# A hybrid encoder layer in float32: seven buffers for the gate's embedding terms, constants in the rows of a weight, squares of x behind its high parts

## The chip, the cores and the metric

The kernel runs on one core of one Trainium2 chip. The metric is the device time of one execution in microseconds (us). The engines are TensorE (PE in the profile, its weight loads PEld), VectorE (DVE), ScalarE (ACT), GpSimd (POOL) and SyncE (SP, which only issues DMAs here).

## The reference, cut to what matters

Sequence 1024, width 1024, one layer. `x` is the residual stream, `p` a per-layer embedding of width 256.

```python
h = rms_norm(x, pre_norm_gain)
q, k, v, z_a, b_gate, c_gate, u, z_c = split(h @ w_in, 8)      # eight parts of 512
attn = diff_attention(q, k, v, lam, slopes)                    # 4 heads, two softmax maps each
attn = rms_norm(attn, subln_gain) * 0.8 * silu(z_a)
conv_out = b_gate * conv3(c_gate * u) * silu(z_c)
mixed = concat(attn, conv_out) @ w_out
x = x + rms_norm(mixed, post_norm_gain)
e = rms_norm(p @ w_ple_proj, ple_norm_gain)
x = x + sigmoid(x @ w_ple_gate) * e
```

## The kernel before, in words

Everything is held transposed: rows of a tile are 128 of the 1024 features (a block `kt` or `m`), its columns 512 positions (a half `n`). Every large product is made in three passes of TensorE: each operand is split into a rounded high part (a cast on ACT, line 89 or 92) and the rest (a subtraction on DVE or POOL, line 90 or 93), and `mm3` (lines 99 to 102) adds high by high, high by rest and rest by high in PSUM. A product of one 128-wide block of outputs with one half of the positions is 8 x 3 = 24 matmuls of 512 columns.

**Order of the work.** The program is written in stages, and a scheduler of the compiler, with a model of the engines' times, sets the order of the instructions on each engine and queue from it: what is written first goes first when its operands are there by the model. On the chip each engine then keeps that order and waits at the head of its queue.

**First stage** (lines 290 to 350). PE runs nine matmuls of zeros. Three pieces of `w_ple` (blocks 0, 1 to 3 and 4 to 7; `load_ple`, line 304) and the two halves of `p` (`load_p`, line 309) are loaded by SP into the pool `rawp`, which has three buffers under the tag `raw`, and split. `embed(n)` multiplies them: 8 blocks of 6 matmuls per half, 96 in all, each block evacuated by ACT (odd `m`, line 326) or DVE (even `m`, line 328) and stored to `e_dram`. A small array of constants (18.5 KB, gains and convolution weights) is loaded by line 343 into `sm`; the splits of x need its columns. `load_x(n)` (line 299) loads the eight blocks of x of a half and splits them, scaled with `col(C_PRE, kt)`, into `hT`; `splits[n, kt]` keeps the two instructions. Then come the weights `wq` and `wk` of head 0 from `w_in`, through `raw` buffers too. Weights lie in the pool `wp`, three buffers under the tag `w` (line 125).

**Second stage.** `row_scale(n)` (line 366) squares the eight blocks of x on ACT (lines 359 and 362, tile `sqx`), adds them on DVE (line 363), sums over the rows with a small matmul (`column_sums`, lines 105 to 117, tile `ms`) and takes the inverse root on POOL (line 97, tile `rsx`); the result `R[n]` is spread over the rows by DVE (line 120). Products of `hT` with a weight are made before the scale is known; their evacuations multiply by `R[n]`. `run` at lines 376 to 378 makes q and k for half 0 (PSUM tag `p`, two banks), q and k for half 1 (tag `s`, three banks) and then the gate z with tag `p` again.

**Middle.** The values, four heads of attention interleaved with the convolution's products (`PLAN`), and `embed_scale`, which leaves the inverse roots for e in `rs_e`.

**Last stage** (from line 486). `out_half(m, n)` multiplies by `w_out`, `post(n, r)` norms, adds x and splits the result into `x1`. `gate_half(m, n)` (line 545), 16 times, loads `e` (line 550, back from `e_dram`, tag `e`, three buffers), scales it on DVE (line 551), multiplies `w_gate` by `x1` on PE (24 matmuls; for the last one two pieces of 256 columns), takes the tanh on ACT (line 560, tile `tg`, two buffers), forms `e = (tg + 1) * e` and `e = e + mix` on DVE (lines 561, 562) and stores `e` from SP to the output (line 563). A buffer of `e` is free for the next load when its store has landed.

Of the kernel before, what the change touches and what calls it, by code (L numbers as in the profile page):

```python
# [12 lines left out]
F32 = mybir.dt.float32  # L13
F32R = mybir.dt.float32r
# [6 lines left out]
P = 128  # L21
# [3 lines left out]
KT = D // P  # L25
HALF = 512
# [14 lines left out]


@with_exitstack
def hybrid_layer(ctx, tc, xT, pT, w_in, small, lams, w_out, w_ple, w_gate, outT):
    nc = tc.nc
    V, A, T, G = nc.vector, nc.scalar, nc.tensor, nc.gpsimd
    mult, add, sub = ALU.mult, ALU.add, ALU.subtract
# [4 lines left out]
    wp = ctx.enter_context(tc.tile_pool(name="wp", bufs=3))  # L52
    rawp = ctx.enter_context(tc.tile_pool(name="rawp", bufs=3))
# [15 lines left out]
    def bank_t(name):  # L69
        return ps_s.tile([P, HALF], F32, tag="t", bufs=2, name=name)  # L70
# [7 lines left out]
    sm = small_c[:, 20:57]  # L78
# [5 lines left out]
    def col(base, k):  # L84
        return sm[:, base + k:base + k + 1]

    def split(hi, lo, src, scale=None, lo_eng=None):
        if scale is None:
            A.copy(out=hi, in_=src)  # L89
            (lo_eng or V).tensor_tensor(out=lo, in0=src, in1=hi.bitcast(F32), op=sub)  # L90
        else:
            return (A.activation(out=hi, in_=src, func=AF.Copy, scale=scale),
                    V.scalar_tensor_tensor(out=lo, in0=src, scalar=scale, in1=hi.bitcast(F32), op0=mult, op1=sub))
# [61 lines left out]
    with ExitStack() as st:  # L155
# [134 lines left out]
        with ExitStack() as st0:  # L290
            sp = st0.enter_context(tc.tile_pool(name="sp", bufs=1))
            s2 = st0.enter_context(tc.tile_pool(name="s2", bufs=2))

            wph = sp.tile([P, KT, 2, P], F32R, name="wph")
            wpo = sp.tile([P, KT, 2, P], F32R, name="wpo")

            splits = {}

            def load_x(n):
                for kt in range(KT):  # L300
                    nc.sync.dma_start(out=mix[kt][n], in_=xT[n, kt])
                    splits[n, kt] = split(hT[n][kt][:, 0], hT[n][kt][:, 1], mix[kt][n], col(C_PRE, kt))

            def load_ple(c):
                raw = rawp.tile([P, c.stop - c.start, 2, P], F32, tag="raw", name="rawe")
                nc.sync.dma_start(out=raw, in_=w_ple[:, c])
                split(wph[:, c], wpo[:, c], raw)

            def load_p(n):
                pth = s2.tile([P, 2, HALF], F32R, tag="pth", name="pth")  # L310
                pto = s2.tile([P, 2, HALF], F32R, tag="pto", name="pto")
                raw = rawp.tile([P, 2, HALF], F32, tag="raw", name="rawt")
                for k in range(2):
                    nc.sync.dma_start(out=raw[:, k], in_=pT[:, n, k])
                    split(pth[:, k], pto[:, k], raw[:, k])
                return pth, pto

            def embed(n, p):
                pth, pto = p
                for m in range(KT):  # L320
                    ps = bank_t("ple") if m % 3 else ps_a.tile([P, HALF], F32, tag="a", name="ple")
                    for k in range(2):
                        mm3(ps, wph[:, m, k], wpo[:, m, k], pth[:, k], pto[:, k], k == 0, k == 1)
                    e = s2.tile([P, HALF], F32, tag="e", bufs=5, name="e")
                    if m % 2:
                        A.copy(out=e, in_=ps)
                    else:
                        V.tensor_copy(out=e, in_=ps)
                    nc.sync.dma_start(out=e_dram[n, m], in_=e)


            zero = sp.tile([P, HALF], mybir.dt.bfloat16, name="zero")
            V.memset(zero, 0.0)
            idle = bank_p("idle")
            for _ in range(9):
                T.matmul(out=idle, lhsT=zero[:, :P], rhs=zero, start=True, stop=True)
            load_ple(slice(0, 1))
            pt0 = load_p(0)
            load_ple(slice(1, 4))
            load_ple(slice(4, 8))  # L340
            pt1 = load_p(1)
            embed(0, pt0)
            nc.sync.dma_start(out=sm, in_=small)
            V.tensor_scalar(out=subg, in0=sm[:, C_SUB:C_SUB + 1], scalar1=0.4, scalar2=None, op0=mult)
            load_x(0)
            embed(1, pt1)
            mixing_weight()
            wq = w_in_tile(0, 0, V)
            wk = w_in_tile(1, 0, V)
            load_x(1)  # L350


        with ExitStack() as st0:
            vp = st0.enter_context(tc.tile_pool(name="vp", bufs=1, reuse_waits="tile"))
            v2 = st0.enter_context(tc.tile_pool(name="v2", bufs=2, reuse_waits="tile"))

            def sums_x(n):
                acc = R[n]
                A.activation(out=acc, in_=mix[0][n], func=AF.Square)
                for kt in range(1, KT):  # L360
                    sq = rowp.tile([P, HALF], F32, tag="t", name="sqx")
                    A.activation(out=sq, in_=mix[kt][n], func=AF.Square)
                    V.tensor_tensor(out=acc, in0=acc, in1=sq, op=add)
                return acc

            def row_scale(n):
                r = tiny.tile([P, 16], F32, tag="rs", name="rsx")
                rsqrt(r, column_sums(sums_x(n), rowp, tag="t")[:, :16], D, 1e-6)
                spread(R[n], r)
                for g in range(4):  # L370
                    A.copy(out=r_col[32 * g:32 * g + 32, 4 * n:4 * n + 4], in_=r[32 * g:32 * g + 32, g:16:4])

            head0 = Head(0)
            row_scale(0)
            row_scale(1)
            run([(wq, head0.ev_q), (wk, head0.ev_k)], (0,))
            run([(wq, head0.ev_q), (wk, head0.ev_k)], (1,), bank_s)
            run([(w_in_tile(3, 0, V), head0.ev_z)])
            wv = vp.tile([P, 2, KT, HALF], F32R, name="wv")
            for h in range(H):  # L380
                raw = rawp.tile([P, KT, P], F32, tag="raw", name="raw")
                nc.sync.dma_start(out=raw, in_=w_in[8 + h])
                c = slice(h * P, (h + 1) * P)
                split(wv[:, 0, :, c], wv[:, 1, :, c], raw)
            for j in range(NT):
                c = slice(j % 4 * P, j % 4 * P + P)
                ps = bank_p("v")
                for kt in range(KT):
                    b = hT[j // 4][kt]
                    mm3(ps, b[:, 0, c], b[:, 1, c], wv[:, 0, kt], wv[:, 1, kt], kt == 0, kt == KT - 1)  # L390
                v = v2.tile([P, 2, HALF], F32R, tag="v", name="v")
                split(v[:, 0], v[:, 1], ps, r_col[:, j:j + 1])
                nc.sync.dma_start(out=v_dram[j], in_=v.bitcast(F32))
# [64 lines left out]
        for h in range(H):  # L458
# [5 lines left out]
            for step in PLAN[h]:  # L464
                k, v = step[0], step[1:]
# [20 lines left out]
    with ExitStack() as st:  # L486
        cp = st.enter_context(tc.tile_pool(name="cp", bufs=1, reuse_waits="tile"))
        c2 = st.enter_context(tc.tile_pool(name="c2", bufs=2, reuse_waits="tile"))
        c4 = st.enter_context(tc.tile_pool(name="c4", bufs=4, reuse_waits="tile"))
# [55 lines left out]
        def gate_half(m, n):  # L545
            if len(re) == n:
                re.append(cp.tile([P, HALF], F32, name=f"re{n}"))
                spread(re[n], rs_e[:, 16 * n:16 * n + 16])
            e = c4.tile([P, HALF], F32, tag="e", bufs=3, name="e")
            nc.sync.dma_start(out=e, in_=e_dram[n, m])  # L550
            V.scalar_tensor_tensor(out=e, in0=e, scalar=col(C_PLE, m), in1=re[n], op0=mult, op1=mult)  # L551
            w = weight(KT + m)
            pieces = 2 if (m, n) == (KT - 1, 1) else 1
            step = HALF // pieces
            for c0 in range(0, HALF, step):
                c, o = slice(c0, c0 + step), slice(n * HALF + c0, n * HALF + c0 + step)
                ps = bank()[:, :step]
                product(w, [[b[:, :, c] for b in r] for r in x1], n, ps)
                t = c2.tile([P, HALF], F32, tag="tg", name="tg")[:, :step]
                A.activation(out=t, in_=ps, func=AF.Tanh, scale=0.5)  # L560
                V.scalar_tensor_tensor(out=e[:, c], in0=t, scalar=1.0, in1=e[:, c], op0=add, op1=mult)
                V.tensor_tensor(out=e[:, c], in0=e[:, c], in1=mix[m][n][:, c], op=add)
                nc.sync.dma_start(out=outT[m * P:(m + 1) * P, o], in_=e[:, c])
# [12 lines left out]
        for m in range(1, 6):  # L576
            gate_half(m, 0)
# [42 lines left out]
```

## Time and profile before

| | us |
|---|---|
| runs (3) | 650.86, 652.25, 652.95; median 652.25 |
| the profiled execution: its own time | 651.04 |
| the profiled execution: span from first to last instruction | 649.3 |
| PE busy | 631.8 (97% of the span) |
| DVE busy | 447.8 (69%) |
| ACT busy | 243.7 (38%) |
| POOL busy | 227.0 (35%) |
| granted clock of TensorE, mean | 0.995 of 2.4 GHz |

A busy share is that of the whole span. Matmuls overlap in the pipeline, so the length of one in the profile is more than the distance from one to the next; the distance is what counts for a stream of them. Times in rows are from the start of the span, and a row names the line of the kernel, the tile written and the tiles read.

### The profile page before, as it was taken

To read this page: it belongs to the slowest core of one execution; us is meant where nothing else is said; L and a number is where in the kernel's file an instruction comes from. 1 tells how busy PE (TensorE), PEld (TensorE's weight loads), DVE (VectorE), ACT (ScalarE), POOL (GpSimd) and SP (SyncE) were. 2 spreads that over 40 slices of the span, in tenths; PEclk is the share of its full clock that TensorE was granted. 3 is DMA by queue.
4 is the path that set the end of the run, shared out by engine and by line. 5 is a ranking of instruction groups with operands and counts; after the bars stand their busy time and mean duration, and the time that the engine had idled before them with its cause. 6 is when DMAs were issued, how large, how long until landed. Compare 5 with 4: busy or idle time off the path is not lost.

```text
span 649.3 us, 8064 instructions
## 1 busy us (share of the span) xinstructions
PE 631.8 (97%) x2941; PEld 523.2 (81%) x2941; DVE 447.8 (69%) x821; ACT 243.7 (38%) x442; POOL 227.0 (35%) x114
## 2 busy tenths in 40 slices
PE   7899999999999999999999999999999999999992
PEld 4688888888888888888888888888888888888882
DVE  6968512698786687876886999539881199795233
ACT  6945312334463333543444434114632326231110
POOL 2006100325326544256362132424560379450000
PEclk9999999999999999999999999999999999999997
DMA  8976522310254102352012400113140125143222
GB/s 286 383 279 194 195 86 86 92 58 5 82 145 138 44 34 81 103 158 65 33 49 82 130 33 33 65 34 130 65 163 0 34 73 187 33 145 98 93 86 97
DMA packets 35654, 67.77 MB, mean 104 GB/s; under 512 B 3744, under 2 KB 12448, under 8 KB 35616
## 3 DMA queue, kind: packets, MB, share of 16 engines
q1 hardware_dynamic: 35616, 67.27, 31.5%
q8 instruction: 23, 0.38, 0.2%
q14 instruction: 15, 0.12, 0.1%
HBM read 48.38 MB, written 12.58 MB: 94 GB/s over the span
## 4 chain that ended last, share of the span: by engine, by line
PE 71%; DVE 12%; DMA 9%; ACT 3%; issue 2%; POOL 2%; DVEq 0%; POOLq 0%; ACTq 0%
PE pj L100 14%; PE pj L102 14%; PE pj L101 14%; PE s L237 5%; DMA e<-e_dram 4%; DMA out_dram<-e 3%; DVE mix L539 3%; PE o L102 3%; PE o L100 3%; PE o L101 3%; PE tpw L264 2%; PE v L100 2%; PE v L101 2%; PE v L102 2%; DVE x L90 2%
## 5 line engine op out<-in xcount | busy, mean ns | idle before, releaser
L100 PE MATMUL pj<-hT,w 128*128 128x512 f32 x448 | 176.4, 394 | 1.2 <-ACT w L89 1.2
L101 PE MATMUL pj<-hT,w 128*128 128x512 f32 x448 | 176.2, 393 | 0.0
L102 PE MATMUL pj<-hT,w 128*128 128x512 f32 x448 | 176.1, 393 | 0.0
L90 POOL TENSOR_TENSOR w<-raw,w 128x1024 fp32r<-128x1024 f32 x41 | 105.5, 2582 | 146.6 <-ACT w L89 143.8
L100 PEld LDWEIGHTS pj<-hT,w 128*128 128x128 f32 x448 | 84.2, 188 | 18.1 <-ACT w L89 2.0
L102 PEld LDWEIGHTS pj<-hT,w 128*128 128x128 f32 x448 | 84.2, 188 | 16.4
L101 PEld LDWEIGHTS pj<-hT,w 128*128 128x128 f32 x448 | 84.2, 188 | 16.1
L245 ACT ACTIVATE p<-p,nm 128x128 f32<-128x128 f32 (+7 forms) x64 | 49.4, 772 | 70.6 <-DVE nm L241 60.7
L89 ACT CAST w<-raw 128x1024 fp32r<-128x1024 f32 x44 | 45.9, 1048 | 21.2 <-issue 11.6
L102 PE MATMUL o<-x,w 128*128 128x512 f32 (+1 forms) x136 | 51.3, 377 | 0.0
L100 PE MATMUL o<-x,w 128*128 128x512 f32 (+1 forms) x136 | 51.2, 377 | 0.0
L101 PE MATMUL o<-x,w 128*128 128x512 f32 (+1 forms) x136 | 51.2, 377 | 0.0
L100 PE MATMUL o<-mT,w 128*128 128x512 f32 x128 | 49.8, 389 | 0.0
L101 PE MATMUL o<-mT,w 128*128 128x512 f32 x128 | 49.8, 389 | 0.0
L102 PE MATMUL o<-mT,w 128*128 128x512 f32 x128 | 49.7, 390 | 0.0
L237 PE MATMUL s<-ks,qs 128*128 128x512 f32 (+2 forms) x192 | 47.5, 346 | 0.0
L89 ACT CAST wt<-tpw 128x512 fp32r<-128x512 f32 (+3 forms) x48 | 21.1, 479 | 60.1 <-PE tpw L264 60.0
L90 DVE TENSOR_TENSOR wt<-tpw,wt 128x512 fp32r<-128x512 f32 (+3 forms) x48 | 25.3, 551 | 26.2 <-ACT wt L89 26.1
L551 DVE SCALAR_TENSOR_TENSOR e<-e,small_c,re 128x512 f32<-128x512 f32 x16 | 16.3, 1017 | 36.5 <-DMA e<-e_dram 36.5
L241 DVE CUSTOM_DVE_ANT_0 p<-s,bias 128x512 f32<-128x512 f32 (+3 forms) x64 | 34.8, 564 | 9.3 <-PE s L237 5.4
L237 PEld LDWEIGHTS s<-ks,qs 128*128 128x128 f32 x192 | 33.4, 188 | 5.0
L405 POOL TENSOR_TENSOR mix<-mix,R 128x512 f32<-128x512 f32 x8 | 12.3, 1543 | 68.6 <-DVE mix L404 66.4
(139 smaller groups left out, 1117.6 us busy)
## 6 DMA issues: line engine op xcount, KB each, us to landing
raw<-in_w_in SPq DMA_DIRECT2D x32, 512.0 KB, 3.6
mix<-in_xT SPq DMA_DIRECT2D x16, 256.0 KB, 6.6
e_dram<-e SPq DMA_DIRECT2D x16, 256.0 KB, 5.6
mix<-e_dram SPq DMA_DIRECT2D x16, 256.0 KB, 3.1
ks<-ks SPq DMA_DIRECT2D x16, 256.0 KB, 3.5
v_dram<-v SPq DMA_DIRECT2D x8, 512.0 KB, 2.6
vs<-v_dram SPq DMA_DIRECT2D x32, 128.0 KB, 2.7
raw<-in_w_out SPq DMA_DIRECT2D x8, 512.0 KB, 3.2
```

Of the source, the lines that this page charges most:

```text
L89: A.copy(out=hi, in_=src)
L90: (lo_eng or V).tensor_tensor(out=lo, in0=src, in1=hi.bitcast(F32), op=sub)
L100: T.matmul(out=ps, lhsT=ah, rhs=bh, start=first, stop=False)
L101: T.matmul(out=ps, lhsT=ah, rhs=bl, start=False, stop=False)
L102: T.matmul(out=ps, lhsT=al, rhs=bh, start=False, stop=last)
L237: T.matmul(out=banks[m][:, :nn], lhsT=s.qs[:, m, qi], rhs=s.ks[:, m, part, c], start=part == 0, stop=part == 1)
L241: V.tensor_tensor_reduce(out=pr[m][:, c0:c0 + n], in0=banks[m][:, :n], in1=s.bias[:, b0:b0 + n], scale=-1.0, scalar=low[m], op0=add, op1=A ...
L245: A.activation(out=pr[m][:, :W], in_=pr[m][:, :W], func=AF.Exp, scale=-1.0, bias=low[m], accum_out=l[:, m:m + 1])
L264: T.transpose(out=tp[:, ii * P:(ii + 1) * P], in_=s.ws[ii][:, j * P:(j + 1) * P], identity=ident)
L405: G.tensor_tensor(out=o, in0=o, in1=R[n], op=mult)
L539: V.scalar_tensor_tensor(out=o, in0=o, scalar=col(C_POST, kt), in1=S1, op0=mult, op1=mult)
L551: V.scalar_tensor_tensor(out=e, in0=e, scalar=col(C_PLE, m), in1=re[n], op0=mult, op1=mult)
```

## The change

It has four parts. The tag `e` gets seven buffers in place of three. The first piece of `w_ple` is loaded on ACT's DMA queue instead of SP's. The constants no longer have an array and a load of their own: they are 37 more columns in the rows of the second piece of `w_ple`, from where DVE copies them to `sm`. The raw halves of `p` no longer take buffers of `raw`; both halves lie in one buffer of the tag `w`. `load_p(1)` is written behind `embed(0, pt0)`. And the instructions of `row_scale(n)` that run on ACT are tied behind `splits[n, KT - 1][0]`, the cast of the last high part of x of that half.

```diff
-            def load_ple(c):
-                raw = rawp.tile([P, c.stop - c.start, 2, P], F32, tag="raw", name="rawe")
-                nc.sync.dma_start(out=raw, in_=w_ple[:, c])
-                split(wph[:, c], wpo[:, c], raw)
+            def load_ple(c, o, queue=nc.sync, constants=0):
+                n = (c.stop - c.start) * 2 * P
+                raw = rawp.tile([P, n + constants], F32, tag="raw", name="rawe")
+                queue.dma_start(out=raw, in_=w_ple[:, o:o + n + constants])
+                if constants:
+                    V.tensor_copy(out=sm, in_=raw[:, n:])
+                split(wph[:, c], wpo[:, c], raw[:, :n].rearrange("p (a b c) -> p a b c", b=2, c=P))
...
-                raw = rawp.tile([P, 2, HALF], F32, tag="raw", name="rawt")
+                raw = p_raw[:, n].bitcast(F32).rearrange("p (k a) b -> p k (a b)", k=2)
...
-            load_ple(slice(0, 1))
+            p_raw = wp.tile([P, 2, KT, P], F32R, tag="w", name="p_raw")
+            load_ple(slice(0, 1), 0, nc.scalar)
             pt0 = load_p(0)
-            load_ple(slice(1, 4))
-            load_ple(slice(4, 8))
+            load_ple(slice(1, 4), 256, constants=37)
+            load_ple(slice(4, 8), 1024 + 37)
+            embed(0, pt0)
             pt1 = load_p(1)
-            embed(0, pt0)
-            nc.sync.dma_start(out=sm, in_=small)
...
-            row_scale(0)
-            row_scale(1)
+            for n in range(2):
+                with tc.issue_after(splits[n, KT - 1][0].ins):
+                    row_scale(n)
...
-            e = c4.tile([P, HALF], F32, tag="e", bufs=3, name="e")
+            e = c4.tile([P, HALF], F32, tag="e", bufs=7, name="e")
...
-        "small": c(small),
...
-        "w_ple": c(blocks(w_ple_proj).transpose(1, 0, 2, 3)),
+        "w_ple": c(np.concatenate([ple[:, :1024], small, ple[:, 1024:]], axis=1)),
```

`ple` is `w_ple_proj` in the same blocks as before, laid out as 128 rows of 2048 columns.

## Rows read from the trace of the kernel before

**Rows 1.** Windows: from:to, length, busy us (count) by engine, PEclk, DMA share, GB/s

```profile
637.52:649.30 11.78, 0.00 (x0) 0.00 (x0) 4.35 (x9) 0.77 (x2) 0.00 (x0) 0.70 0.30 111
...
5.83:25.73 19.90, 16.81 (x64) 11.50 (x65) 18.34 (x34) 18.05 (x31) 0.00 (x0) 1.00 1.01 364
25.73:637.52 611.79, 611.55 (x2869) 510.57 (x2867) 423.05 (x773) 222.60 (x407) 222.53 (x105) 1.00 0.29 95
```

**Rows 2.** The chain that ended last, its end: start, us, what

```profile
637.13 1.99 DMA out_dram<-e
639.13 2.54 DMA e<-e_dram
...
641.80 0.75 DVE e L551
...
645.64 0.42 DVE e L562
```

**Rows 3.** Waits, whole span: engine, line, releaser: us in total, times, longest

```profile
DVE e L551 <- DMA e<-e_dram: 36.5, 11, 4.2
...
DVE acc L523 <- ACT sqo L522: 24.8, 6, 4.7
```

**Rows 4.** Timeline of ACT, last stage: start, us, instruction [idle before it]

```profile
610.03 0.60 ACT L560 ACTIVATE tg<-o 128x512 f32<-128x512 f32 x1 [4.84 <-PE o L102]
615.48 0.60 ACT L560 ACTIVATE tg<-o 128x512 f32<-128x512 f32 x1 [4.84 <-PE o L102]
...
637.80 0.38 ACT L560 ACTIVATE tg<-o 128x256 f32<-128x256 f32 x1 [5.40 <-DVE e L561]
```

**Rows 5.** Timeline of DVE, start of the last stage

```profile
467.52 2.88 DVE L551 SCALAR_TENSOR_TENSOR e<-e,small_c,re 128x512 f32<-128x512 f32 x1
...
481.57 0.74 DVE L551 SCALAR_TENSOR_TENSOR e<-e,small_c,re 128x512 f32<-128x512 f32 x1
```

**Rows 6.** Timeline of POOL, the same stretch

```profile
462.27 18.82 POOL L90 TENSOR_TENSOR w<-raw,w 128x1024 fp32r<-128x1024 f32 x7 [9.77 <-ACT w L89]
```

**Rows 7.** Waits of PE, whole span

```profile
PE ple L100 <- ACT e L326: 1.1, 2, 0.9
...
PE pj L100 <- ACT w L89: 1.2, 2, 0.7
```

**Rows 8.** Windows of line 362 alone (ACT): squares of x before head 0's weights

```profile
8.77:23.70 14.93, 4.37 (x7) 1.00 1.02 376
```

**Rows 9.** Timeline of SP, first stage: start and length of DMA issues

```profile
0.72 0.39 SPq L306 DMA_DIRECT2D rawe<-in_w_ple  x1
1.17 0.90 SPq L314 DMA_DIRECT2D rawt<-in_pT  x2
```

**Rows 10.** Windows of the first stage, columns as in the first group

```profile
4.00:6.00 2.00, 0.82 (x4) 0.27 (x2) 1.49 (x6) 0.62 (x1) 1.00 (x1) 1.00 1.03 271
...
8.00:10.00 2.00, 1.50 (x7) 0.83 (x6) 1.32 (x3) 2.00 (x3) 0.00 (x0) 1.00 1.01 395
```

**Rows 11.** Timeline of DVE, first and second stage

```profile
8.15 0.15 DVE L344 TENSOR_SCALAR small_c<-small_c 128x1 f32<-128x1 f32 x1 [0.59 <-DMA small_c<-in_small]
...
9.71 0.68 DVE L328 COPY e<-ple 128x512 f32<-128x512 f32 x1
...
18.17 0.69 DVE L90 TENSOR_TENSOR pto<-rawt,pth 128x512 fp32r<-128x512 f32 x1
...
35.06 0.68 DVE L109 TENSOR_REDUCE part<-flip 128x16 f32<-128x512 f32 x1
...
53.74 0.68 DVE L194 SCALAR_TENSOR_TENSOR tq<-pj,R 128x512 f32<-128x512 f32 x1
```

**Rows 12.** Timeline of ACT: the third weight's cast

```profile
31.71 1.05 ACT L89 CAST w<-raw 128x1024 fp32r<-128x1024 f32 x1 [0.44 <-DMA raw<-in_w_in]
```

**Rows 13.** Timeline of PE, second stage: the sum over the rows

```profile
46.59 0.29 PE L116 MATMUL ms<-part,fold 128*128 128x16 f32 x2
```

**Rows 14.** Tile pj, 20 to 70 us: duration ns min/median/max, first and last start

```profile
L102 PE MATMUL pj<-hT,w x48: 389/389/476, 26.2 to 65.9; 128*128 128x512 f32 x48
```

More of the change, by code (lines that the diff above doesn't have):

```diff
@@ L43, in hybrid_layer @@
 @with_exitstack
-def hybrid_layer(ctx, tc, xT, pT, w_in, small, lams, w_out, w_ple, w_gate, outT):
+def hybrid_layer(ctx, tc, xT, pT, w_in, lams, w_out, w_ple, w_gate, outT):
     nc = tc.nc
@@ L602 @@
     ], axis=1)
+    ple = blocks(w_ple_proj).transpose(1, 0, 2, 3).reshape(P, -1)
     arrays = {
```

## The prediction

> **What bounds the kernel now.** I read the windows first, cut where PE changes its state. From 25.73 to 637.52 us PE is busy 611.55 of 611.79 us: there it is the bound, and nothing that the change touches takes work from it. What can be won lies outside: in front, 19.90 us that hold only 64 matmuls, and behind, 11.78 us in which PE does nothing [rows 1]. Next, the end of the chain of waits: the last 40 us don't go through PE at all but round a loop of DVE and DMA. An output block is stored (1.99 us), the freed buffer is loaded with the next e (2.54), DVE scales that e (0.75), and the next store follows [rows 2]. The list of waits says the same of DVE: 36.5 us at line 551 for e's load, in 11 waits [rows 3]. One pass of the loop takes 1.99 + 2.54 + 0.75 and line 562's some 0.65, 5.9 us and a few gaps, while PE ends a product every 5.45 us (tanh at 610.03 and 615.48, each after a wait for PE) [rows 2, 4]. So DVE falls behind PE by some 0.5 us a block, until the last blocks are finished long after the last product. At 637.80 even the tanh waits for DVE, through its two buffers [rows 4]. PE itself is not held up: it has banks enough.
>
> **The end of the kernel: seven buffers.** With seven, e's load waits for the store of seven blocks earlier, 7 x 5.45 = 38 us, against 1.99 + 2.54 us for store and load: that wait is gone. DVE then has per block 0.75 us (line 551) and for lines 561 and 562 at most twice 0.84 (double what line 562 takes on 256 columns), 2.4 us against PE's 5.45, so it keeps up. What is late next is PE itself: behind its last matmul at 637.52 stand one tanh of 256 columns (0.38), lines 561 and 562 on 256 columns (0.42 each, the row of line 562 taken for both), and the last store. I take the store and the wait for it as now: line 562 ends at 645.64 + 0.42 = 646.06 and the span at 649.30, 3.24 us. 637.52 + 0.38 + 0.42 + 0.42 + 3.24 = 642.0. **The end gains 7.3 us** [rows 1, 2, 4]. The bound above is that; below, if DVE's order leaves one block of line 551, 561, 562 in front of the last piece, 2 us less.
>
> The four more loads move forward, and so do four scalings. The three that have buffers today already run before 482, and there one of them took 2.88 us against 0.74 for the one at 481.57 [rows 5]; POOL subtracts weights from 462.27 to 481.09 [rows 6], and the short one starts after that. So four more scalings cost DVE between 4 x 0.74 = 3.0 and 4 x 2.88 = 11.5 us in that stretch, if the order puts them there. I take nothing on the path: DVE has idle time behind that stretch, when it only adds one square per product: 24.8 us of waits at line 523, up to 4.7 us each [rows 3]. The upper end is a rival below. The Trainium skill (SBUF — State Buffer, "Who interferes with whom") has a rule that speaks against the earlier scalings: a DVE instruction with two SBUF inputs and a GpSimd instruction that reads SBUF block each other for a whole instruction. By it the sum would be that of the rival with its 2.88 us a block; the trace agrees, as the 2.88 and the 0.74 show.
>
> **The start.** First what is there to win. One matmul of a stream takes 5.45 / 24 = 0.227 us, so 64 take 14.5, and 19.90 - 14.5 = 5.4 us are lost between the first matmul of the embedding (5.83) and steady work [rows 1].
>
> *Squares behind the high parts.* In 8.77 to 23.70 us ACT is busy almost throughout and spends 4.37 us on seven squares of x [rows 8]; the sums of them on DVE stand likewise among the splits that PE waits for. Both leave this stretch. They are not saved but done later, beside PE's products. What they delay is in PE's waits: 1.1 us for embedding blocks that ACT has not yet evacuated, and 1.2 us for the casts of head 0's weights [rows 7], 2.3 us together. I take these 2.3. The lower end is 0, for the DMA engines are taken at a share of 1.01 in 5.83 to 25.73 [rows 1]: if x and the weights land no earlier, ACT only waits for them instead. The upper end is the whole 5.4.
>
> *First piece on ACT's queue.* SP begins `p` at 1.17 instead of 0.72, as it issues the piece first [rows 9]; without it `p` starts 0.45 us earlier, and the first matmul waits for `p`. ACT has nothing to do at that moment but to get its table, and the piece is needed no earlier than `p`. I take 0.45. Could more transfers in flight give more? At 4 to 6 us the DMA engines are as busy as at 8 to 10 (1.03 and 1.01) but move 271 GB/s instead of 395 [rows 10]; over 4 us that is 124 x 4 = 0.5 MB, 1.3 us at the higher rate. That is the upper end, the lower is 0. The Trainium skill (DMA: Bandwidth & Descriptors, "Issuing engines are not separate DMA queues") says that transfers issued from several engines interleave on the same 16 DMA engines and only issue time is saved. By it the sum stands as it is, with the 0.45; by the difference of rates it would be about 0.9 us lower.
>
> *The constants and the raw `p`.* One DMA of 18.5 KB goes, and its bytes travel in the second piece. DVE copies 128x37: between 0.15 us (128x1) and 0.68 (128x512) [rows 11], nearest to the first, and DVE still waits for data at that time. The third piece of `w_ple` no longer waits for a `raw` buffer, which is part of the rates above. The raw halves hold one of three `w` buffers until the last split of `p` (18.86 today [rows 11]); the third weight is cast at 31.71 [rows 12]. No cost, with 12.8 us to spare. `load_p(1)` behind `embed(0)` in the text costs nothing as long as SP has it issued before the embedding's stores; its four rows are needed only for the second half of the embedding.
>
> *What the moved squares may cost.* q of half 0 is evacuated when R[0] is there: line 194 ends at 53.74 + 0.68 = 54.42 [rows 11]. PE wants that bank for the gate z. The six products that begin in 20 to 70 us end with the matmul at 65.9 [rows 14], and z's two are the last, so z begins at about 65.9 + 0.23 - 48 x 0.227 = 55.2: only 0.8 us to spare. If PE comes 2.75 us earlier and R[0] does not, PE waits 2 us there and most of the start's gain is given back. But the sums behind R[0] are ready at 35.06 + 0.68 = 35.74, and the small matmul that takes them stands in PE's own order at 46.59 [rows 11, 13]. The chain from there to 54.42 (7.8 us) moves forward with PE, and the squares may come 10 us later without being late. I take nothing; the end of the range is 7.8 us, if the order puts that matmul right in front of z.
>
> **The sum.** 649.3 - 7.3 - 2.3 - 0.45 = 639.25 us of span. The profiled execution lay 1.74 us above its span (651.04), which gives 641.0; the median of the runs is 652.25, 1.21 above that execution, so the runs after should have a median of **642.2 us**. A measurement of this kernel can tell about 0.3% (2 us) from no change.
>
> **Rivals.**
>
> 1. *The start gives nothing or takes some.* The data bounds it, or PE waits for R[0] at z. For it: a DMA share of 1.01 and only 0.8 us to spare. Against it: 10 us between the ready sums and the matmul. 642.2 + 2.75 = 645.0 if the data takes the start's gain; 642.2 + 7.8 = 650.0 at the worst if PE waits at z. Chance 0.15.
> 2. *The whole of the start is won.* All 5.4 + 0.45 us, as more transfers are in flight and ACT and DVE are lighter: 642.2 - 3.1 = 639.1. For it: the rates. Against it: some gaps are waits for data and for DVE, which stay. Chance 0.08.
> 3. *The change does not do what it says at the end.* The order on DVE or SP still ties one block's scaling to another's store, as now, so that only the start is won: 642.2 + 7.3 = 649.5. Against it: nothing else than the buffer makes the load wait for the store. Chance 0.04.
> 4. *Slower: scalings beside POOL in front of PE's operands.* Place: 462 to 481 us, where DVE also makes the rests of the first operands for `w_out`. Price: 4 x 2.88 = 11.5 us of DVE. If all four stand in front of a rest that PE is waiting for, PE idles that long: 642.2 + 11.5 = 653.7. It decides from the fourth on: three (8.6 us) leave 650.8. For it: the 2.88 [rows 5]. Against it: the splits are written earlier than the scalings, so they go first when ready, and three scalings already stand there without a wait of PE. Chance 0.03.
>
> **How the numbers follow.** The forecast as summed has 0.70: 640.2 (1.3 of rates and 0.7 of noise) to 645.0. The range is to hold 8 in 10; it takes in rival 2 and the likelier half of rival 1: 639.0 to 646.8. Faster by over 0.3% are the forecast, rivals 1 and 2, and half of rival 3: 0.95, less a little for stalls in a new order of the middle, 0.94. Within 0.3%: the rest of rival 3 and of that, 0.03. Slower: 0.03.
>
> **What the profile after would show.** Right: no wait of DVE line 551 for e's load in the last 60 us; tanh every 5.45 us to the end, and none that waits for line 561; 4 to 5 us from the last matmul to the end of the span instead of 11.78; squares of half 0 all behind the last high part of x; waits of PE for ACT before head 0's weights under 1 us; PE steady from about 23. Wrong, if PE shows a gap near z (50 to 56 us) released by R[0]'s chain; if line 551 still waits; or if PE idles between 462 and 482.

## The result, and the profile after

The changed kernel took 643.30 us (median of 4 runs, 642.96 to 644.44) beside 652.10 before (650.86 to 652.95): a ratio of 0.987, 95% interval 0.9849 to 0.989. Forecast were 642.2, 639.0 to 646.8. Measured again later on one chip with its variants it gave 645.66 (5 runs, 643.18 to 646.34), ratio 0.9906 (0.989 to 0.9921). Both lie in the range. The profiled execution took 644.44, with a span of 642.6; it is the longest of the first four, while that of before was near the shortest of its own. So the two traces differ by 6.7 us of span and the medians by 8.8. Why the two medians of the same kernel lie 2.4 us apart is not shown; the last section has what the traces say of it.

The windows of the kernel after, cut like those of before [rows 1] (columns as there):

```profile
5.88:25.26 19.38, 17.64 (x66) 13.45 (x67) 16.64 (x34) 16.36 (x28) 0.00 (x0) 0.91 1.04 394
25.26:638.14 612.88, 611.41 (x2867) 510.16 (x2865) 429.00 (x781) 223.80 (x412) 222.92 (x105) 1.00 0.29 96
638.14:642.60 4.46, 0.00 (x1) 0.00 (x0) 0.85 (x2) 0.38 (x1) 0.00 (x0) 1.00 0.08 29
```

Behind the last matmul there are 4.46 us instead of 11.78: 7.3 us less, as summed. The last matmul itself ends at 638.14 instead of 637.52: of the start's 2.75 us nothing has arrived in this trace. And between the two, PE is no longer without gaps: 1.47 us of 612.88 are idle.

The waits of the kernel after, over the whole span (the counterpart of [rows 3]), show that the step on the buffers was wrong in its reason:

```profile
DVE e L555 <- DMA e<-e_dram: 19.8, 7, 4.2
```

The scaling (line 555 now) still waits for its load, 7 times instead of 11, and still up to 4.2 us at a time. DVE's timeline of the kernel after shows how:

```profile
605.70 0.75 DVE L555 SCALAR_TENSOR_TENSOR e<-e,small_c,re 128x512 f32<-128x512 f32 x1 [4.06 <-DMA e<-e_dram]
606.36 0.68 DVE L566 TENSOR_TENSOR e<-e,mix 128x512 f32<-128x512 f32 x1
606.97 0.69 DVE L565 SCALAR_TENSOR_TENSOR e<-tg,e 128x512 f32<-128x512 f32 x1
611.84 0.75 DVE L555 SCALAR_TENSOR_TENSOR e<-e,small_c,re 128x512 f32<-128x512 f32 x1 [4.19 <-DMA e<-e_dram]
...
617.89 0.75 DVE L555 SCALAR_TENSOR_TENSOR e<-e,small_c,re 128x512 f32<-128x512 f32 x1 [4.10 <-DMA e<-e_dram]
...
619.16 0.68 DVE L565 SCALAR_TENSOR_TENSOR e<-tg,e 128x512 f32<-128x512 f32 x1
619.88 0.69 DVE L566 TENSOR_TENSOR e<-e,mix 128x512 f32<-128x512 f32 x1
620.49 0.68 DVE L565 SCALAR_TENSOR_TENSOR e<-tg,e 128x512 f32<-128x512 f32 x1
621.21 0.69 DVE L566 TENSOR_TENSOR e<-e,mix 128x512 f32<-128x512 f32 x1
...
627.62 0.69 DVE L565 SCALAR_TENSOR_TENSOR e<-tg,e 128x512 f32<-128x512 f32 x1 [4.02 <-ACT tg L564]
```

Between two of these scalings SP issues one store and one load:

```profile
607.08 0.34 SPq L567 DMA_DIRECT2D out_dram<-e  x1
609.10 0.32 SPq L554 DMA_DIRECT2D e<-e_dram  x1
```

Look at the distance of one scaling from the next: 6.14 and 6.05 us, with seven buffers as with three. A block's scaling stands in DVE's order right ahead of the last operation (line 566) on an earlier block. That operation ends at 607.04, its store is issued at 607.08, and the load of the next scaling's e only at 609.10, when the store has freed the buffer. So the next scaling can't come before store and load have followed, and with this order the loop was there with three, four and seven buffers alike. With seven, the sixteenth load is issued four blocks earlier: the last scaling runs at 617.89 instead of 641.80 [rows 2]. Behind it DVE has only operations whose data is there; it makes up its lag at once (619.16 to 622.9) and from then on waits for ACT, that is for PE.

### The profile page after: what moved, and what is told of

Its sections match the earlier page's. It is cut to its first block, busy times and chain, and to the rows that moved or that the text cites. A ratio compares the mean times of both kernels' runs of the same rounds, so it can differ in the third digit from the quotient of the medians.

```text
span 642.6 us, 8062 instructions
## 1 busy us (share of the span) xinstructions
PE 632.9 (98%) x2941; PEld 524.8 (82%) x2941; DVE 448.5 (70%) x822; ACT 242.7 (38%) x442; POOL 227.4 (35%) x114
## 4 chain that ended last, share of the span: by engine, by line
PE 90%; POOL 2%; ACT 2%; DVE 2%; DMA 2%; issue 1%; SPq 0%; POOLq 0%; DVEq 0%; ACTq 0%
PE pj L100 14%; PE pj L102 14%; PE pj L101 14%; PE o L102 9%; PE o L100 9%; PE o L101 9%; PE s L237 5%; PE tpw L264 2%; PE v L100 2%; PE v L101 2%; PE v L102 2%; PE av L102 1%; PE av L101 1%; POOL mix L446 1%; PE av L100 1%; DMA rawe<-in_w_ple 1%
## 5 line engine op out<-in xcount | busy, mean ns | idle before, releaser
L253 DVE SCALAR_TENSOR_TENSOR p<-p,rl,p 128x128 f32<-128x128 f32 (+7 forms) x32 | 32.7, 1022 | 0.4
```

Source lines behind the costliest of these rows:

```text
L253: V.scalar_tensor_tensor(out=pr[0][:, :W], in0=pr[1][:, :W], scalar=rl, in1=pr[0][:, :W], op0=mult, op1=add)
```

## The experiments

Each was timed against the kernel before on the same chip. The last column is the distance from the end of the last matmul to the end of the span in the profiled execution. A comparison's runs of the kernel before had medians of 651.8 (the first four), 651.56 (the second four) and 652.14 (the last three).

| kernel | median us | ratio, 95% interval | last matmul ends | behind it |
|---|---|---|---|---|
| end7_only | 644.44 | 0.9884 (0.9868 to 0.99) | 638.37 | 4.6 |
| start_only | 652.87 | 1.0015 (1.0 to 1.0029) | 639.08 | 12.1 |
| late_scale3 | 643.90 | 0.988 (0.9861 to 0.9899) | 637.12 | 4.6 |
| end4 | 646.99 | 0.9924 (0.9909 to 0.994) | 637.66 | 8.0 |
| after_again | 645.66 | 0.9906 (0.989 to 0.9921) | 636.91 | 4.5 |
| no_tie | 645.52 | 0.9907 (0.9892 to 0.9922) | 639.03 | 4.5 |
| piece0_on_sp | 644.60 | 0.9895 (0.9878 to 0.9911) | 638.19 | 4.5 |
| hold_wv | 643.71 | 0.9877 (0.9863 to 0.989) | 636.98 | 4.5 |
| best | 644.67 | 0.988 (0.9864 to 0.9896) | 636.30 | 4.6 |
| after_zeros13 | 643.11 | 0.9863 (0.9847 to 0.988) | 636.72 | 4.6 |
| best_zeros13 | 643.69 | 0.9868 (0.9854 to 0.9883) | 637.26 | 4.5 |

**The two halves of the change, apart.**

The kernel before with seven buffers alone (end7_only):

```diff
-            e = c4.tile([P, HALF], F32, tag="e", bufs=3, name="e")
+            e = c4.tile([P, HALF], F32, tag="e", bufs=7, name="e")
```

> The kernel before with seven buffers of e and nothing else. Theory A (the end's gain is all in the buffers, and the start gives the small rest): 7.3 us less than before, 11.78 us behind the last matmul become about 4.5, a median near 644.8. Theory B (the start's edits are what moved the median, the buffers less): over 647. In the trace, by A in its later form (DVE's fixed order is what makes the scaling wait, and more buffers only let the loop of store, load and scaling end earlier), the scaling of e goes on waiting for its load, some 19 us in all, until the last load is in; by the prediction's form (seven buffers end the wait) there is no such wait.

It took 644.44: 7.4 us less than before, and no more than 1.2 us from either median of the whole change. Its waits at line 551 come to 20.5 us in 7. Theory A holds, and in its later form.

The changed kernel with three buffers again (start_only, the same line the other way round):

> The changed kernel with three buffers of e again, so the start's edits alone. Theory A: the end is as before (about 11.8 us behind the last matmul), the start is worth 8.8 - 7.3 = 1.5 us, a median of 650 to 651. The prediction's sums: 2.75 us, 649.4. Theory B: 647 or less.

It took 652.87, not less than before. The start's edits by themselves give no gain. Here, though, the loop of store, load and scaling sets the end and not PE, so a small gain of PE could hide behind it; that is why the start's variants below were made with seven buffers.

**What makes the scaling wait.**

late_scale3 leaves the kernel before its three buffers and only keeps DVE from placing a scaling ahead of the block before:

```diff
+        done = []
...
-            V.scalar_tensor_tensor(out=e, in0=e, scalar=col(C_PLE, m), in1=re[n], op0=mult, op1=mult)
+            with (tc.issue_after(done[-1].ins) if done else ExitStack()):
+                V.scalar_tensor_tensor(out=e, in0=e, scalar=col(C_PLE, m), in1=re[n], op0=mult, op1=mult)
...
-                V.tensor_tensor(out=e[:, c], in0=e[:, c], in1=mix[m][n][:, c], op=add)
+                done.append(V.tensor_tensor(out=e[:, c], in0=e[:, c], in1=mix[m][n][:, c], op=add))
```

> The kernel before, still three buffers, but DVE scales e of a block only behind the last operation on the block before it. If DVE's order causes the wait (the scaling stands ahead of operations whose store frees its own buffer), the wait is gone with three buffers too: no wait of the scaling for e's load over 1 us in the last 50 us, about 4.5 us behind the last matmul, a median near 644.8. If three buffers are too few for the loop, as the prediction had it, the waits stay and the median stays at 652.

643.90, 7.9 us less than before, with three buffers. In DVE's timeline of this kernel (line 553 scales, 563 and 564 are the two operations behind the tanh) the scaling follows the block before and finds its data there; the only waits are for ACT:

```profile
611.61 0.74 DVE L553 SCALAR_TENSOR_TENSOR e<-e,small_c,re 128x512 f32<-128x512 f32 x1
615.71 0.69 DVE L563 SCALAR_TENSOR_TENSOR e<-tg,e 128x512 f32<-128x512 f32 x1 [3.36 <-ACT tg L562]
616.44 0.69 DVE L564 TENSOR_TENSOR e<-e,mix 128x512 f32<-128x512 f32 x1
617.05 0.74 DVE L553 SCALAR_TENSOR_TENSOR e<-e,small_c,re 128x512 f32<-128x512 f32 x1
```

The distance of two scalings is 5.44 us, PE's pace. The expectation was missed in one point: five waits are left, 7.2 us in all and up to 2.6 each, some of them within the last 50 us, but they lie before 608 and don't reach the end. So three buffers are enough, and DVE's order is what makes the loop.

end4 is the kernel before with four buffers:

> The kernel before with four buffers of e. If a buffer more gives the load the time it needs (4 x 5.45 us against 4.5 us for store and load), there is no wait of the scaling left. If DVE's order makes the loop, its period of about 6 us stays and the waits stay near 30 us in all, the last load lands one block earlier (some 6 us), and DVE catches up most of its lag behind it: 4.5 to 6 us behind the last matmul, a median of 645 to 646.5.

646.99, and the waits of the kernel with four buffers are nearly those of three:

```profile
DVE e L551 <- DMA e<-e_dram: 33.3, 10, 4.3
```

Its DVE after the last load:

```profile
636.75 0.75 DVE L551 SCALAR_TENSOR_TENSOR e<-e,small_c,re 128x512 f32<-128x512 f32 x1 [4.21 <-DMA e<-e_dram]
...
641.93 0.42 DVE L562 TENSOR_TENSOR e<-e,mix 128x256 f32<-128x256 f32 x1
```

The last scaling comes 5 us earlier than with three buffers (636.75 instead of 641.80) and DVE works 5.6 us without a pause behind it, past the end of the last matmul at 637.66. So it ends at 642.35, 3.7 us earlier. The lag is made up only partly, less than was expected (8.0 us behind the last matmul instead of 4.5 to 6). The median, 646.99, lies above the expected 645 to 646.5 for the same reason. The theory of the order is confirmed by the waits; the theory of "time for the load" would have had none.

**Where the start's gain went.**

after_again is the changed kernel unchanged:

> The changed kernel once more, beside its variants: about 643.3, ratio 0.987. In its trace PE waits about 1 us at the gate z for the evacuation of q (line 194), whatever the clock does in the first 12 us.

It took 645.66, 2.4 us more than the first time, with executions from 643.18 to 646.34. Its profiled execution, 643.18, is the shortest of its five and one with TensorE at full pace early on. To see how far ahead PE is, take the first low-by-high matmul of q's product (line 102), which has 66 or 67 matmuls of the embedding and of q in front of it with either start. Here it is in the kernel before and, below, in after_again:

```profile
26.18 0.39 PE L102 MATMUL pj<-hT,w 128*128 128x512 f32 x1
```

```profile
23.73 0.39 PE L102 MATMUL pj<-hT,w 128*128 128x512 f32 x1
```

With the old start it comes at 25.87 to 26.18 in three traces (before, end4, late_scale3), so PE is 2.1 to 2.5 us ahead, near the 2.75 that were summed. In the first trace of the changed kernel, with a low clock until about 12 us (last section), it comes at 25.26, and at 26.79 in end7_only, which has the old start and the low pace too: 1.5 us. PE's waits in the trace of after_again show what is lost behind it:

```profile
PE pj L100 <- DVE tq L194: 1.1, 1, 1.1
PE ple L100 <- ACT e L329: 0.9, 1, 0.9
PE ms L116 <- DVE part L109: 0.8, 1, 0.8
```

PE now waits 1.1 us at the gate z for q's evacuation. It also waits 0.8 us for the second sum over rows (0.4 in the kernel after); with the old start that wait is 0.2 in the kernel before, but 0.5 in end7_only and 0.7 in end4, so most of it is not the start's doing. The wait at z is the same in the kernel after; these are its rows of PE and, below, of DVE:

```profile
47.48 0.29 PE L116 MATMUL ms<-part,fold 128*128 128x16 f32 x2
...
55.55 0.50 PE L100 MATMUL pj<-hT,w 128*128 128x512 f32 x1 [1.07 <-DVE tq L194]
```

```profile
51.94 0.71 DVE L120 STREAM_TRANSPOSE R<-rsx 128x512 f32<-128x512 f32 x1 [0.99 <-POOL rsx L97]
52.57 2.32 DVE L90 TENSOR_TENSOR wv<-raw,wv 128x1024 fp32r<-128x1024 f32 x2
54.81 0.68 DVE L194 SCALAR_TENSOR_TENSOR tq<-pj,R 128x512 f32<-128x512 f32 x1
```

The sums behind R[0] are ready at 38.74 (their row of before is in [rows 11]), 8.7 us before the matmul that takes them. The matmul stands at 47.48 in PE's order and only 7.0 us before z would have begun (55.55 less the wait, 54.48), where before there were 8.6 (55.2 - 46.59). The chain from it to the end of q's evacuation takes 8.0 us, before 7.8. So z waits by its place in the order, and not because PE came early: the wait is 1.07 us in after, where that matmul of line 102 comes at 25.26, as in after_again with 23.73. That is rival 1's wait at z, by the other of its two ways: not R[0] left behind, but the small matmul nearer to z.

How much is lost can be read without the first 24 us, where the pace of TensorE differs from trace to trace. From that first matmul of line 102 to the end of the last matmul PE takes 611.2 to 611.8 us in the four traces with the old start and no other change to it (before, end7_only, late_scale3, end4), and 612.9 to 613.2 in after, after_again, start_only and no_tie, which all wait at z. So 1.1 to 2 us are given back, 1.1 of them at z. In after_again 0.6 us of the lead are left at the last matmul (636.91 against 637.52); in after the last matmul is 0.6 us late.

no_tie is the changed kernel without the tie of the squares:

```diff
-            for n in range(2):
-                with tc.issue_after(splits[n, KT - 1][0].ins):
-                    row_scale(n)
+            row_scale(0)
+            row_scale(1)
```

> The changed kernel without the tie that puts the squares of x behind the high parts. Theory A (the tie moves PE's first products forward by about 1 us, but the small matmul of R[0] moves back in PE's order, and the gain is lost in a wait of 1.07 us at z): without it no wait at z, the first steady products of hT about 1 us later, the median within 1 us of the changed kernel. Theory B (the tie is worth the 2.3 us of the prediction): 2 us more, about 645.5. Theory C (the tie only costs): 1 us less.

645.52 beside 645.66: the tie is worth nothing that the medians can tell. (Theory B's 645.5 was reckoned from 643.3; beside after_again it asked for 2 us more, which the medians refute.) The wait at z is there without it too (1.1 us in PE's waits), so theory A is wrong in blaming the tie for it. It is right in the other half, as far as one trace each can show: set beside the trace of the kernel after, which also has the low clock early on, the first matmul of line 102 comes 0.7 us later (25.92 against 25.26) and the last matmul ends 0.9 us later (639.03 against 638.14). From the small matmul to z there are 7.0 us here as well, and 7.1 in piece0_on_sp below: neither the tie nor ACT's queue brought it nearer to z. The other edits of the start (the constants' rows, the buffer of the raw `p`, the place of `load_p(1)`) were not tried apart.

piece0_on_sp puts the first piece back on SP:

```diff
-            load_ple(slice(0, 1), 0, nc.scalar)
+            load_ple(slice(0, 1), 0)
```

> The changed kernel with the first piece of w_ple issued by SP again. Theory A (issued by ACT, the piece is put behind the first half of p in ACT's order, so its cast ends at 5.8 and the first matmul gains nothing from the 0.45 us): the cast stands before that of p again, the first matmul comes within 0.3 us of the 5.88 of the changed kernel, the median within 0.5 us. By the prediction's term: 0.45 us slower.

644.60, 1.1 us below after_again, with intervals that overlap (0.9878 to 0.9911 and 0.989 to 0.9921): at least no gain from ACT's queue is seen in the time, and both numbers of the expectation are missed. The first matmul comes at 6.49 here, at 6.40 and 5.88 in the two traces of the changed kernel, at 5.83 before. A reason stands in ACT's timeline of the kernel after:

```profile
4.91 0.62 ACT L89 CAST pth<-p_raw 128x512 fp32r<-128x512 f32 x1 [2.48 <-DMA p_raw<-in_pT]
5.43 0.40 ACT L89 CAST wph<-rawe 128x256 fp32r<-128x256 f32 x1
```

`p` is cast 0.25 us earlier (4.91, before 5.16), but with the piece on ACT's queue the scheduler places the piece's cast behind that of `p`, where before it was done at 3.5. The first matmul waits for the piece's cast now. One pair of traces is little here: over all that were kept, `p` is cast at 4.68 to 5.42 with the piece on ACT's queue (eight traces, 4.9 in the mean) and at 5.16 to 5.82 with it on SP's (five, four of them with the old start, 5.5 in the mean), and the first matmul comes at 5.69 to 6.40 (5.9) and 5.83 to 6.49 (6.2). So `p` is cast some 0.6 us earlier, about as was summed, and 0.3 of it reach the first matmul. In this variant the piece's cast is first again, and the wait of 1.1 us at z is gone too: DVE has one split of the values' weight between R[0] and q's evacuation there, not two, and the evacuation starts at 52.19 (a wait of 1.3 us stands before the values instead). That may be why it is not slower; it was not tried apart.

hold_wv takes up DVE's two splits of the values' weight between R[0] and q's evacuation, 2.32 us in the rows above:

```diff
-                V.scalar_tensor_tensor(out=t, in0=ps, scalar=0.125, in1=R[n], op0=mult, op1=mult)
+                s.tq = V.scalar_tensor_tensor(out=t, in0=ps, scalar=0.125, in1=R[n], op0=mult, op1=mult)
+                if n == 0:
+                    s.tq0 = s.tq
...
-                split(wv[:, 0, :, c], wv[:, 1, :, c], raw)
+                with tc.issue_after(head0.tq0.ins):
+                    split(wv[:, 0, :, c], wv[:, 1, :, c], raw)
```

> The changed kernel with the splits of the values' weight held on DVE behind the first evacuation of q, so that R[0] and that evacuation come first. Theory A (the wait at z is DVE's order: two splits of 2.3 us together stand between R[0] and the evacuation): the evacuation starts at about 52.6 instead of 54.8, no wait at z, 1.1 us less: about 642.2. If the wait has another cause: unchanged.

643.71, 2.0 us below the changed kernel in the same comparison; the two ratios' intervals just touch (0.9863 to 0.989 and 0.989 to 0.9921). In its DVE the evacuation follows R[0] at once:

```profile
51.19 0.71 DVE L120 STREAM_TRANSPOSE R<-rsx 128x512 f32<-128x512 f32 x1
51.94 0.69 DVE L194 SCALAR_TENSOR_TENSOR tq<-pj,R 128x512 f32<-128x512 f32 x1
52.54 3.48 DVE L90 TENSOR_TENSOR wv<-raw,wv 128x1024 fp32r<-128x1024 f32 x3
```

PE's waits hold no entry at z, though the small matmul stands no farther from it (6.8 us). From the first matmul of line 102 to the end of the last one PE takes 611.6 us, as with the old start, instead of 612.9 to 613.2. Theory A is confirmed for the wait: DVE's order lets work that nobody waits for yet go ahead of q's evacuation. It did so in the kernel before too (the same two splits stand at 51.50 there, 2.32 us), where the 8.6 us from the small matmul to z were enough; so the wait takes both, that order and the nearer matmul. How much time that is worth is less sure than the 2.0 us of the medians look: the profiled executions of the two kernels take the same time (643.33 and 643.18), hold_wv's with the low clock early on and after_again's without.

**Versions put together.** best is hold_wv with the later scaling of late_scale3 (seven buffers).

> The changed kernel with the values' weight held behind the first evacuation of q and the scaling of e held behind the block before it (seven buffers). Theory: the first gives what it gave alone (643.7), the second nothing more in time, since with seven buffers DVE had caught up before the end anyway: 643 to 644; in the trace no wait of the scaling over 1 us in the last 50 us and no wait at z. If the loop of store, load and scaling still costs something at the end: 0.5 us less or more.

644.67 (643.02 to 644.84), a little above what was expected. In its trace there is no wait at z and none of the scaling for e's load from 590 us on. Its profiled execution, 643.02, is the shortest of its four and the span of 640.9 the shortest of all that were profiled; the others were near 644.7.

after_zeros13 and best_zeros13 change a number that has nothing to do with the change, 13 matmuls of zeros instead of 9 (`for _ in range(13):`), as the executions' scatter pointed to the first 12 us:

> The changed kernel with 13 matmuls of zeros instead of 9 ahead of the first product, the rest as it is. Theory A (the scatter of the changed kernel between 643 and 646 is TensorE's clock, which in some executions stays at the lower level until about 11 us, since PE has little to do from 5 to 8 us): with work until about 6 us the clock stays up, PE does 6 or 7 matmuls in 8 to 10 us in place of 4, and the median is 1 to 2 us lower than in the last comparison, near 644. Theory B (the zeros don't decide it): unchanged, 645.7, or later by what the zeros delay the first product (up to 0.7 us).

643.11, with executions from 642.90 to 643.55: the least scatter and the lowest ratio of all, 0.9863. In the windows of after_zeros13 in that stretch the granted clock stays at 1.00, with six matmuls in 8 to 10 us:

```profile
4.00:6.00 2.00, 2.00 (x8) 0.74 (x6) 0.47 (x1) 0.92 (x2) 1.00 (x1) 1.00 0.89 293
6.00:8.00 2.00, 1.62 (x4) 0.60 (x4) 1.27 (x4) 0.83 (x2) 0.00 (x0) 1.00 1.01 382
8.00:10.00 2.00, 1.33 (x6) 1.11 (x7) 1.35 (x5) 1.59 (x3) 0.00 (x0) 1.00 1.05 405
```

This fits theory A, but doesn't show it alone: the scheduler also set another order behind, and the wait at z is gone there.

> All three together: by theory A 642 to 643, with executions within 1 us of each other; by theory B as the first of these runs, 643 to 644.

643.69, as theory B had it: no better than after_zeros13. None of the three is clearly below the 643.30 of the changed kernel's first measurement; against after_again alone, after_zeros13 is lower (0.9863 with an upper end of 0.988, to 0.9906 with a lower end of 0.989).

## Why the prediction was right, and where it was wrong

- **The end: right in its size, wrong in its reason.** 7.3 us were summed, 11.78 - 4.46 = 7.3 were found, and 7.4 in end7_only's median. The step "that wait is gone", from 38 us against 4.5, failed: it took each scaling to be placed when it is needed. DVE's order places it ahead of the operation whose store frees the buffer for the next load, so the loop of 6 us stays: 19.8 us in 7 waits, up to 617.89, within the last 60 us where none was to be. That is what rival 3 says of DVE's order, with a chance of 0.04; only its price was wrong. The size came out because DVE's lag only counts at the end: the loop ends four blocks earlier and DVE needs 5 us to make it up. That seven were enough for this is luck, as the prediction did not reckon with it: with four buffers the same reasoning would have been wrong in size too (end4: 4.8 us of gain instead of 7.3). The sum behind the last matmul itself is right to the hundredth: 0.38 + 0.42 + 0.42 + 3.24 = 4.46.
- **Nothing on the path for the earlier scalings: right.** They came beside POOL as feared, six in a row, but behind the splits that PE waits for. This row of DVE after answers to [rows 5]:

```profile
474.90 8.34 DVE L555 SCALAR_TENSOR_TENSOR e<-e,small_c,re 128x512 f32<-128x512 f32 x6
```

That is 1.4 us each instead of 0.74, and PE has no wait there. Rival 4 needed them in front.
- **The start: wrong, 2.75 us forecast, about 0 found.** start_only gives 1.0015, and end7_only, with the old start, lies between the two medians of the whole change. A lead is there at 24 us: 2.1 to 2.5 us in after_again (23.73, against 25.87 to 26.18 with the old start), 1.5 between two traces with the low pace. But it does not come from where the term of 2.3 us was read. Of its two waits, that for an evacuation by ACT stays (0.9 us, before 1.1), and that for the casts of head 0's weights (1.2 us) goes without the tie as well (no_tie); the tie itself is worth some 0.7 us at that place, in one pair of traces. The size of the lead is in part luck. The step that failed is "What the moved squares may cost": the chain to R[0] was taken to keep its distance from z. It did not, since the place of the small matmul in PE's order was set anew, 1.6 us nearer to z, and the 0.8 us to spare were not enough. The prediction named this end of the range ("if the order puts that matmul right in front of z") and took nothing for it; it measured 1.07 us at z in each trace. What the lead is worth beyond that hangs on the pace of the first 12 us. And no_tie, without the tie, has the same median and the same wait.
- **The 0.45 us of the first piece: not found in the time.** Over all traces `p` is cast some 0.6 us earlier, but the piece's own cast is placed behind it, so that only 0.3 reach the first matmul. The prediction had looked at when the piece is needed and not at what its move does to ACT's order.
- **The rate of the DMA engines.** 373 GB/s in 6 to 8 us after (245 before, in the stretch between those of [rows 10]) and 308 in 4 to 6 (271): the higher rate that the prediction kept for its upper end came about. In 6 to 8 us it does not come from the second issuing engine: with the first piece on SP's queue again it is 383 GB/s (piece0_on_sp), and 245 to 298 in the four traces with the old start. That is no case against the Trainium skill's rule (DMA: Bandwidth & Descriptors, "Issuing engines are not separate DMA queues"), that other issuing engines only save issue time. What did change is that loads are issued earlier, the second half of `p` at 2.61 instead of 7.59; that this is the cause was not tried apart. In 4 to 6 us piece0_on_sp has 232, with traces of the old start between 198 and 295: nothing can be told there. The 1.3 us of that upper end are not seen in the time.
- **The sum** was right within 1.1 us of the first median (643.30) and 3.5 of the second, since a term of 7.3 carried it and the wrong one was 2.75. The measured time is that of rival 1's first case (645.0) as much as of the forecast, by its second case's mechanism at a small part of its price. And of the three signs that the prediction itself named for being wrong, two are in the profile after: the gap at z, and line 551's waits.

## What to carry to other kernels

When an engine waits for a load, look at what stands behind the waiting instruction in its order: if that frees the load's buffer, a few buffers more don't end the wait (here with three, four and seven), and placing the consumer later does (here with three buffers as well as with seven). A lag of an engine that isn't the bound costs only what is left of it at the end; count the blocks that remain after the last wait. And a gain in front of a bound engine can be lost at the next hand-over that has little slack, when the change makes the scheduler set the order anew: here the slack between q's evacuation and z went from 0.8 us to -1.0.

## What the runs showed of the hardware that was not expected

TensorE's pace in the first 12 us differs from execution to execution of the same kernel. In the profiled execution after, the granted clock was 0.50 in 8 to 10 us, the lower level of 1.2 GHz, and 0.64 in 10 to 12; PE had done four matmuls in 6 to 8 us, with waits between them. after_again did four there too and kept 1.00, so what decides it is not shown. These are windows of the kernel after, and below them of after_again, the same kernel:

```profile
6.00:8.00 2.00, 1.64 (x4) 0.63 (x4) 1.37 (x4) 1.02 (x2) 0.00 (x0) 1.00 1.00 373
8.00:10.00 2.00, 1.52 (x4) 1.23 (x5) 1.33 (x4) 1.63 (x3) 0.00 (x0) 0.50 1.04 393
10.00:12.00 2.00, 2.00 (x7) 1.60 (x6) 0.55 (x1) 0.88 (x2) 0.00 (x0) 0.64 1.06 409
```

```profile
6.00:8.00 2.00, 1.49 (x4) 0.67 (x4) 1.73 (x4) 1.56 (x4) 0.00 (x0) 1.00 1.00 390
8.00:10.00 2.00, 1.71 (x7) 1.42 (x8) 1.35 (x5) 1.60 (x3) 0.00 (x0) 1.00 1.06 408
10.00:12.00 2.00, 2.00 (x10) 1.65 (x9) 2.00 (x3) 1.81 (x4) 0.00 (x0) 1.00 1.06 407
```

The two executions are 1.5 us apart at 24 us (25.26 and 23.73) and still 1.2 at the last matmul (638.14 and 636.91). The column of the clock doesn't always show it: in end7_only it stands at 1.00 in 8 to 10 us, while matmuls start 0.43 us apart (8.08, 8.51, 8.93) instead of 0.227. These 1.2 us are less than the changed kernel's executions lie apart (642.96 to 646.34), and one of 645.66 has a mean granted clock of 1.000; where the rest comes from is open. So a comparison of the start from one trace of each kernel can be off by more than the edits are worth.
